# Multi-query attention on one core: value products dealt out one by one, more exponentials on VectorE, and part of their last product on GpSimd

## The chip, the cores and the metric

The kernel runs on one core of one Trainium2 chip. The metric is device time in microseconds (us) from start to end of one execution; smaller is better. The core has five engines that matter here: TensorE (PE in the profile; its weight loads are PEld), VectorE (DVE), ScalarE (ACT), GpSimd (POOL) and the queue engine SyncE (SP). Each runs its own list of instructions in order and waits on semaphores for the others.

## The reference

Sixteen query heads share one head of keys and values (batch 8, sequence 1024, head size 64).

```python
q: (8, 1024, 16, 64)   k, v: (8, 1024, 64)      # float32, random normal
scores  = q @ k.T / sqrt(64)                    # for every head
weights = softmax(scores, axis=-1)
out     = weights @ v                           # (8, 1024, 16, 64) float32
```

## The kernel before

The work is cut into steps. A step is one tile of scores: 128 keys (key tile `j`, 8 of them) by 512 queries (chunk `c`, 2 of them) for a pair of heads (`p`, 64 pairs over all batches), so 64 x 2 x 8 = 1024 steps. The tile is 128 partitions (keys) by 1024 columns (2 heads x 512 queries) and lies in PSUM, in one of three buffers `sc`. In each step `scores` has PE make the tile with two matmuls, and then one of two engines takes its exponential:

- ScalarE, in one instruction (line 260), into a float16 tile `wt`.
- VectorE, in every fifth step (`to_vector`, `VE_EVERY = 5`), in a unit of five instructions (`vector_exp`). The first (line 211) reads the scores from PSUM and writes an int16 whose bits, read as float16, are a straight-line approximation of the power. The next ones, from and to SBUF, take its mantissa `m` (line 217) and its power of two (line 227), square the mantissa (line 235, into `m2`) and multiply (line 237) the approximation by that square. The result is three tiles in one buffer `w3` (six buffers), which are added up by PE with values that are scaled by three constants. So a ScalarE tile needs one value product for each group of queries and a VectorE tile three.

The value products are in `values`: for a group `g` of 128 queries of one head (8 groups to a block of 8 steps, 1024 groups in all) it emits all products of that group over the 8 key tiles at once, 8 and two more for each VectorE tile among them. Seven groups share a PSUM bank. When a bank is full, `inverse` (line 263, reciprocal of the sums) and `finish` (line 272, scaling, then a store to memory) are put on the list `late`, and from there at the head of VectorE's list `pend`.

The order is written out by hand. The main loop runs over batches of two steps: for both steps scores and exponential, with two instructions taken from `pend` after each step; then the products of two groups whose tiles were made at least 16 steps before (`LAG`); then the loads and preparations for later batches (`after`). The last product of a unit (line 237) is held in `product` and joins `pend` behind the first instruction of the next unit. From step `HURRY` on (12 steps from the end) up to four groups follow each batch. `last_values` makes the products of the very last block, key tile by key tile, when all else is emitted.

GpSimd issues the loads of q (line 121) and v (line 104), and twice per batch of the input scales and converts K (line 190). SP issues K loads, transposes of q and K, and the stores.

Of the kernel before, what the change touches and what calls it, by code (L numbers as in the profile page):

```python
# [14 lines left out]
ALU = mybir.AluOpType  # L15
# [6 lines left out]
C0 = 0.9833984375  # L22
C3 = 0.163818359375
CS = 2.1471603163479376
VE_EVERY = 5


@with_exitstack
def attention_main(ctx, tc, q, k, v, out, flag):
# [11 lines left out]
    nc = tc.nc  # L41
    B, S, H, D = q.shape
    P = 128
    NKT = S // P
    QCH = 512
    NCH = S // QCH
    HP = H // 2
    NP = B * HP
    NQB = QCH // P
    GRP = 2 * NQB  # L50
    NG = NP * NCH * GRP
    GB = 7
# [15 lines left out]
    op = ctx.enter_context(tc.tile_pool(name="op", bufs=2, space=PSUM))  # L68
# [9 lines left out]
    kv = {}  # L78
    q16 = {}
    qt = {}  # L80
    wt = {}
    osb = {}
    ot = {}
    pend = []
    product = []
    late = []
# [48 lines left out]
    def bank(name):  # L135
        return op.tile([P, 512], FP32, tag="ot", name=name)
# [69 lines left out]
    def vector_exp(sc, p, c, j):  # L206
        w3 = w3p.tile([P, 3, 2, QCH], FP16, tag="w3", name=f"we{p}_{c}_{j}")
        m = mp.tile([P, 2, QCH], FP16, tag="m", name=f"m{p}_{c}_{j}")
        m2 = mp.tile([P, 2, QCH], FP16, tag="m2", name=f"mm{p}_{c}_{j}")
        t = w3[:, 1].bitcast(I16)  # L210
        nc.vector.tensor_scalar(  # L211
            out=t, in0=sc, scalar1=15.0 * 1024, scalar2=0.0, op0=ALU.add, op1=ALU.max
        )
        if product:
            pend.append(product.pop())
        pend.append(
            lambda: nc.vector.tensor_scalar(  # L217
                out=m.bitcast(I16),
                in0=t,
                scalar1=0x3FF,  # L220
                scalar2=0x3C00,
                op0=ALU.bitwise_and,
                op1=ALU.bitwise_or,
            )
        )
        pend.append(
            lambda: nc.vector.tensor_scalar(  # L227
                out=w3[:, 0].bitcast(I16),
                in0=t,
                scalar1=0x7C00,  # L230
                scalar2=None,
                op0=ALU.bitwise_and,
            )
        )
        pend.append(lambda: nc.vector.tensor_tensor(out=m2, in0=m, in1=m, op=ALU.mult))  # L235
        product.append(
            lambda: nc.vector.tensor_tensor(out=w3[:, 2], in0=w3[:, 1], in1=m2, op=ALU.mult)  # L237
        )
        wt[(p, c, j)] = [(w3[:, 0], 1), (w3[:, 1], 0), (w3[:, 2], 2)]

# [21 lines left out]
    def inverse(o, g0, n):  # L262
        nc.vector.reciprocal(out=rec_all[:, g0 : g0 + n], in_=o[:, 0:n, D])  # L263

    def finish(o, g0, n):

        rec = rec_all[:, g0 : g0 + n]
        i0 = g0 % (OCH * GRP)
        if i0 == 0:
            osb[0] = osbp.tile([P, OCH * GRP, D], FP32, tag="osb", name=f"osb{g0}")  # L270
        ob = osb[0]
        nc.vector.tensor_tensor(  # L272
            out=ob[:, i0 : i0 + n, :],
            in0=o[:, 0:n, 0:D],
            in1=rec.unsqueeze(2).broadcast_to([P, n, D]),
            op=ALU.mult,
        )
        while stored[0] < g0 + n:
            e = stored[0]
            e += GRP // 2 if e >= NG - GRP else GRP  # L280
            if e > g0 + n:
                break
            store(ob, stored[0], e)
            stored[0] = e
        per = HP * NCH * GRP
        if g0 + n == NG:
            check(g0 - GRP // 2, NG, ok_all[:, B:])
        elif checked[0] < B and g0 + n >= min((checked[0] + 1) * per, NG - GRP):
            e = min((checked[0] + 1) * per, NG - GRP)
            b = checked[0]  # L290
            check(b * per, e, None, ok_all[:, b : b + 1])
            checked[0] += 1

    def store(ob, g0, g1):
        p, c = divmod(g0 // GRP, NCH)
        b, hp = divmod(p, HP)
        q0 = c * QCH + g0 % GRP // 2 * P
        j0 = g0 % (OCH * GRP)
        n = g1 - g0
        nc.sync.dma_start(  # L300
            out=out[b, q0 : q0 + n // 2 * P, 2 * hp : 2 * hp + 2, :].rearrange(
                "(qb p) h d -> p qb (h d)", p=P
            ),
            in_=ob[:, j0 : j0 + n, :].rearrange("p (qb h) d -> p qb (h d)", h=2),
        )

    def values(p, c, g):

        b = p // HP
        qb, hh = divmod(g, 2)  # L310
        gg = (p * NCH + c) * GRP + g
        if gg % GB == 0:
            ot[0] = bank(f"ot{gg}")[:, 0 : GB * 72].rearrange("p (g f) -> p g f", f=72)
        o = ot[0]
        vp = kv[b]["vp"]
        terms = [(j, w, i) for j in range(NKT) for w, i in wt[(p, c, j)]]
        for n, (j, w, i) in enumerate(terms):
            nc.tensor.matmul(  # L318
                o[:, gg % GB, 0 : D + 1],
                w[:, hh, qb * P : (qb + 1) * P],  # L320
                vp[:, i, j, 0 : D + 1],
                start=(n == 0),
                stop=(n == len(terms) - 1),
            )
        if gg % GB == GB - 1 or gg == NG - GRP - 1:
            late.append((o, gg - gg % GB, gg % GB + 1))
        if g == GRP - 1:
            for j in range(NKT):
                del wt[(p, c, j)]

    def last_values():

# [39 lines left out]
    LAG = 2 * NKT + 2  # L372
    STEPS = NP * NCH * NKT
    PSTEPS = NCH * NKT
    BATCH = 2
    LAST_VE = (STEPS - 2 * NKT) // VE_EVERY * VE_EVERY
    HURRY = STEPS - NKT - 4

    def to_vector(u):
        return u % VE_EVERY == 0 and NKT <= u <= LAST_VE  # L380

    def step(u):
        p, r = divmod(u, PSTEPS)
        c, j = divmod(r, NKT)
        scores(p, c, j, to_vector(u))
        for _ in range(2):
            if pend:
                pend.pop(0)()
        if product and u >= LAST_VE + 2 and not pend:
            product.pop()()  # L390

    def after(u):
        p, r = divmod(u, PSTEPS)
# [24 lines left out]
    with tc.manual_schedule():  # L418
        load_kv(0)
        load_q_first(0)  # L420
        make_identity(nc, ident)
        for p in range(1, NFIRST):
            load_q_first(p)
        load_v(0)
        for c in range(NKT):
            load_q(0, c)
        for t in vps:
            for i, ci in enumerate((1.0, C0, C3)):
                nc.gpsimd.memset(t[:, i, :, D : D + 1], ci)
        nc.vector.tensor_copy(out=ident16, in_=ident)  # L430
        nc.vector.memset(ones, 1.0)
        kps = bank("kps0").bitcast(FP16)
        turned[0] = bank("qps0").bitcast(FP16)
        lo, hi = range(NKT // 2), range(NKT // 2, NKT)
        q0 = q16[("first", 0)]
        nc.scalar.copy(out=q0[:, 0 : NKT // 2, :], in_=qf[:, 0 : NKT // 2, :])  # L436
        first_k(kps, 0)
        first_q(turned[0], 0, lo)
        first_q_out(turned[0], 0, lo, nc.scalar.copy)
        first_k_out(kps, 0)  # L440
        first_k(kps, 1)
        first_k_out(kps, 1)
        nc.vector.tensor_copy(out=q0[:, NKT // 2 :, :], in_=qf[:, NKT // 2 :, :])
        prep_v(0)
        for c in range(NKT):
            turn_q(0, c)
        nxt = 0
        for u0 in range(0, STEPS, BATCH):
            us = range(u0, u0 + BATCH)
            for u in us:  # L450
                step(u)
            for f in late:
                pend.insert(0, lambda f=f: inverse(*f))
                pend.insert(min(2, len(pend)), lambda f=f: finish(*f))
            del late[:]
            for _ in range(2 * BATCH):
                if u0 < HURRY:
                    ready = nxt < u0 + BATCH - LAG
                else:
                    ready = nxt < STEPS - GRP and nxt // GRP * NKT + NKT + 4 <= u0  # L460
                if ready:
                    pa, ra = divmod(nxt, PSTEPS)
                    values(pa, *divmod(ra, NKT))
                    nxt += 1
            for u in us:
                after(u)
        assert nxt == STEPS - GRP
        assert not product
        for f in pend:
            f()  # L470
        for f in late:
            inverse(*f)
            finish(*f)
        last_values()
        okm = chkp.tile([P, 1], FP32, tag="okm", name="okm")
        nc.vector.tensor_reduce(out=okm, in_=ok_all, axis=AX.X, op=ALU.min)
        cnt = bank("cnt")[0:1, 0:1]
        nc.tensor.matmul(cnt, okm, ones, start=True, stop=True)
        nc.vector.tensor_scalar(
            out=flag, in0=cnt, scalar1=P - 0.5, scalar2=None, op0=ALU.is_lt  # L480
        )
# [120 lines left out]
```

## Time and profile before

| | us |
|---|---|
| median of 3 runs | 782.24 (781.58 to 783.35) |
| the profiled execution | 783.46 |
| its span, first to last instruction | 781.5 |

| engine | busy us | share of the span |
|---|---|---|
| PE | 728.7 | 93% |
| VectorE | 728.9 | 93% |
| ScalarE | 762.5 | 98% |
| GpSimd | 65.9 | 8% |

A group's row names line, engine and operation, what is written from what, the number of instructions, their busy time and the mean duration of one, and behind the second bar the engine's idle time just before them with what ended it. In the timeline a row begins with start and duration. VectorE's instructions overlap at their edges, so a mean is longer than the distance from one start to the next. The PE clock granted was 0.99 over the run.

### The profile page before, as it was taken

What the parts mean: (1) busy time and instruction counts of PE and PEld (TensorE: products, weight loads), DVE (VectorE), ACT (ScalarE), POOL (GpSimd) and SP (SyncE); (2) the same over time, 40 slices, a digit from 0 to 9 for tenths busy, and PEclk for the clock granted to TensorE, in tenths of its full rate; (3) what the DMA queues carried; (4) which work ended last, traced back from release to release, by engine and by line L of the source; (5) the groups of instructions that cost most, each with busy time, mean ns of one, the idle gap of its engine ahead of it and who ended that gap; (6) DMA issues with size and microseconds to landing.
All of it is one profiled execution on the core that took longest, in us unless ns stands there. A gap on an engine that the chain in (4) does not pass through costs nothing.

```text
span 781.5 us, 30669 instructions
## 1 busy us (share of the span) xinstructions
PE 728.7 (93%) x13474; PEld 474.1 (61%) x13474; DVE 728.9 (93%) x1349; ACT 762.5 (98%) x827; POOL 65.9 (8%) x99
## 2 busy tenths in 40 slices
PE   5999999999999999999999999999999999999996
PEld 2566666656666666666656666666666666666665
DVE  3899999999999999999999999999999999999992
ACT  7999999999999999999999999999999999999996
POOL 4210002100011002010020100201002100000000
PEclk8899999999999999999999999999999999999999
DMA  9949118582193813756155552556417373111113
GB/s 169 146 93 164 55 44 157 97 136 57 29 170 76 154 33 76 150 103 115 45 91 123 124 95 56 90 128 115 101 42 125 89 149 71 51 35 55 43 43 84
DMA packets 168633, 73.84 MB, mean 94 GB/s; under 512 B 93744, under 2 KB 161328, under 8 KB 168496
## 3 DMA queue, kind: packets, MB, share of 16 engines
q1 hardware_dynamic: 148864, 53.76, 32.5%
q0 software_dynamic: 18576, 17.57, 14.8%
q8 instruction: 106, 1.74, 1.0%
q10 hardware_dynamic: 1056, 0.52, 0.3%
q14 instruction: 31, 0.25, 0.1%
HBM read 37.75 MB, written 33.55 MB: 91 GB/s over the span
## 4 chain that ended last, share of the span: by engine, by line
ACT 38%; DVE 21%; PE 21%; issue 19%; DMA 1%; DVEq 0%; ACTq 0%
ACT wt L260 38%; PE ot L318 11%; PE sc L247 9%; DVE we L211 8%; DVE osb L272 3%; DVE we L237 3%; DVE mm L235 3%; DVE m L217 2%; DVE we L227 2%; DVE rec_all L263 1%; DMA qf<-in_q_dram 1%; PE otl L344 0%; DVE both L366 0%; DVE ok_all L370 0%; DVE ge L360 0%
## 5 line engine op out<-in xcount | busy, mean ns | idle before, releaser
L260 ACT ACTIVATE wt<-sc 128x1024 f16<-128x1024 f32 x824 | 760.0, 1062 | 7.4 <-PE sc L247 6.1
L318 PE MATMUL ot<-vp,wt 128*128 128x65 f16 x6528 | 418.4, 194 | 0.6 <-issue 0.6
L318 PEld LDWEIGHTS <-wt 128*128 128x128 f16 x6528 | 325.8, 98 | 114.8 <-issue 114.8
L247 PE MATMUL sc<-qt,k2t 64*128 64x512 f16 x2048 | 352.8, 386 | 41.2 <-ACT wt L260 29.1
L318 PE MATMUL ot<-vp,we 128*128 128x65 f16 x4800 | 352.2, 193 | 0.0
L318 PEld LDWEIGHTS <-we 128*128 128x128 f16 x4800 | 250.0, 97 | 30.6 <-issue 30.6
L211 DVE TENSOR_SCALAR we<-sc 128x1024 int16<-128x1024 f32 x200 | 243.6, 1218 | 23.2 <-PE sc L247 22.1
L247 PEld LDWEIGHTS <-k2t 64*128 64x128 f16 x2048 | 93.2, 94 | 149.0 <-issue 111.0
L237 DVE TENSOR_TENSOR we<-we,mm 128x1024 f16<-128x1024 f16 x200 | 136.9, 685 | 0.0
L235 DVE TENSOR_TENSOR mm<-m 128x1024 f16<-128x1024 f16 x200 | 136.5, 683 | 0.0
L272 DVE TENSOR_TENSOR osb<-ot,rec_all 128x448 f32<-128x448 f32 x146 | 90.5, 620 | 4.2 <-DVE rec_all L263 0.2
L217 DVE TENSOR_SCALAR m<-we 128x1024 int16<-128x1024 int16 x200 | 85.8, 429 | 0.0
L227 DVE TENSOR_SCALAR we<-we 128x1024 int16<-128x1024 int16 x200 | 83.5, 418 | 0.0
L104 POOL DMA_DIRECT2D vp<-in_v_dram x8 | 7.5, 936 | 388.5 <-PE ot L318 388.4
L121 POOL DMA_DIRECT2D q<-in_q_dram x64 | 35.0, 571 | 26.7 <-DMA qt<-q 22.9
L263 DVE RECIPROCAL rec_all<-ot 128x7 f32<-128x7 f32 x146 | 28.6, 196 | 8.7 <-PE ot L318 8.6
L190 POOL TENSOR_SCALAR k16d<-knat 128x512 f16<-128x512 f32 x14 | 21.4, 1537 | 134.7 <-DMA knat<-in_k_dram 134.7
L202 DVE TENSOR_SCALAR vp<-vp 128x512 f16<-128x512 f16 x16 | 3.9, 286 | 2.0 <-DMA vp<-in_v_dram 2.0
L155 PE MATMUL kps<-ident,k 128*64 128x128 f16 x16 | 1.3, 314 | 4.5 <-DVE k L146 4.5
L184 DVE COPY qt<-qps 128x512 f16<-128x512 f16 (+1 forms) x2 | 1.1, 554 | 3.3 <-PE qps L171 3.3
L155 PEld LDWEIGHTS <-k 128*64 128x64 f16 x16 | 0.8, 159 | 4.7 <-DVE k L146 4.7
L436 ACT ACT_TABLE_LOAD x1 | 1.3, 1283 | 1.9 <-issue 1.9
(29 smaller groups left out, 22.2 us busy)
## 6 DMA issues: line engine op xcount, KB each, us to landing
out_dram<-osb SPq DMA_DIRECT2D x127, 256.0 KB, 2.4
q<-in_q_dram POOLq DMA_DIRECT2D x56, 256.0 KB, 8.8
knat<-in_k_dram SPq DMA_DIRECT2D x7, 256.0 KB, 4.1
q<-in_q_dram POOLq DMA_DIRECT2D x8, 192.0 KB, 8.0
vp<-in_v_dram POOLq DMA_DIRECT2D x8, 128.0 KB, 4.4
qt<-q SPq DMA_TRANSPOSE x64, 3.9
qf<-in_q_dram ACTq DMA_DIRECT2D x2, 256.0 KB, 4.4
knat<-in_k_dram SPq DMA_DIRECT2D x2, 128.0 KB, 3.8
```

Of the source, the lines that this page charges most:

```text
L121: nc.gpsimd.dma_start(out=q16[(b, c)], in_=q[b, c * P : (c + 1) * P, h0:, :].rearrange("p h d -> p (h d)"),)
L190: nc.gpsimd.tensor_scalar(out=k16d[:, :, i, :], in0=st["knat"], scalar1=kscale, scalar2=None, op0=ALU.mult)
L211: nc.vector.tensor_scalar(out=t, in0=sc, scalar1=15.0 * 1024, scalar2=0.0, op0=ALU.add, op1=ALU.max)
L217: lambda: nc.vector.tensor_scalar(out=m.bitcast(I16), in0=t, scalar1=0x3FF, scalar2=0x3C00, op0=ALU.bitwise_and, op1=ALU.bitwise_or,)
L227: lambda: nc.vector.tensor_scalar(out=w3[:, 0].bitcast(I16), in0=t, scalar1=0x7C00, scalar2=None, op0=ALU.bitwise_and,)
L235: pend.append(lambda: nc.vector.tensor_tensor(out=m2, in0=m, in1=m, op=ALU.mult))
L237: lambda: nc.vector.tensor_tensor(out=w3[:, 2], in0=w3[:, 1], in1=m2, op=ALU.mult)
L247: nc.tensor.matmul(sc[:, hh, :], k2t[r : r + 64, j * P : (j + 1) * P], qt[b][r : r + 64, p % HP, c * QCH : (c + 1) * QCH], start=True, sto ...
L260: nc.scalar.activation(out=w, in_=sc, func=EXP, scale=escale, bias=math.log(CS))
L263: nc.vector.reciprocal(out=rec_all[:, g0 : g0 + n], in_=o[:, 0:n, D])
L272: nc.vector.tensor_tensor(out=ob[:, i0 : i0 + n, :], in0=o[:, 0:n, 0:D], in1=rec.unsqueeze(2).broadcast_to([P, n, D]), op=ALU.mult,)
L318: nc.tensor.matmul(o[:, gg % GB, 0 : D + 1], w[:, hh, qb * P : (qb + 1) * P], vp[:, i, j, 0 : D + 1], start=(n == 0), stop=(n == len(terms ...
```

## The change

- Units: of 41 steps 9 go to VectorE, so 4 or 5 steps lie between units (5 before); there are 220 in place of 200, up to step 1007 (1005 before).
- The last product of a unit is split by columns. VectorE keeps the first 384 of 1024. The other 640 go to GpSimd, in an instruction that is issued with the square and waits for it.
- The value products are dealt one by one. `values` now returns a list of single products; `plan` works out how many should have been emitted after each batch: more after a batch with two ScalarE tiles (about 35), fewer after one with a VectorE tile (about 9), with a correction of an eighth towards the group that is due. A group may begin two steps earlier than before (`AHEAD`), and its products may go over from one batch to the next. Before, a batch had two whole groups, 20 or 24 products.
- When one bank is finished, the first waiting entry of `pend` stands between its reciprocal and its scaling, as before.
- The end: `HURRY` begins 14 steps before the end (12 before), and a block may follow 2 steps earlier, so that the last batch of steps has no products behind it.

```diff
-VE_EVERY = 5
+VE_U = 384
+VE_N = 9
+VE_M = 41
...
-        pend.append(lambda: nc.vector.tensor_tensor(out=m2, in0=m, in1=m, op=ALU.mult))
+        we, wu, mm = (x.rearrange("p h q -> p (h q)") for x in (w3[:, 1], w3[:, 2], m2))
+
+        def square():
+            nc.vector.tensor_tensor(out=m2, in0=m, in1=m, op=ALU.mult)
+            nc.gpsimd.tensor_tensor(
+                out=wu[:, VE_U:], in0=we[:, VE_U:], in1=mm[:, VE_U:], op=ALU.mult
+            )
+
+        pend.append(square)
         product.append(
-            lambda: nc.vector.tensor_tensor(out=w3[:, 2], in0=w3[:, 1], in1=m2, op=ALU.mult)
+            lambda: nc.vector.tensor_tensor(
+                out=wu[:, :VE_U], in0=we[:, :VE_U], in1=mm[:, :VE_U], op=ALU.mult
+            )
         )
...
-    def values(p, c, g):
+    def values(gg):
...
-        for n, (j, w, i) in enumerate(terms):
+        def one(n, j, w, i):
+            last = n == len(terms) - 1
             nc.tensor.matmul(
...
+        return [lambda n=n, t=t: one(n, *t) for n, t in enumerate(terms)]
...
-    LAST_VE = (STEPS - 2 * NKT) // VE_EVERY * VE_EVERY
-    HURRY = STEPS - NKT - 4
+    OTHER = 21
+    AHEAD = 2
+    LAST_VE = max(u for u in range(STEPS - 2 * NKT + 1) if u * VE_N % VE_M < VE_N)
+    HURRY = STEPS - NKT - 6
 
     def to_vector(u):
-        return u % VE_EVERY == 0 and NKT <= u <= LAST_VE
+        return NKT <= u <= LAST_VE and u * VE_N % VE_M < VE_N
...
+    def plan():
+        at = range(LAG, HURRY, BATCH)
+        tiles = [sum(not to_vector(u) for u in range(u0, u0 + BATCH)) for u0 in at]
+        upto = [0]
+        for g in range(HURRY - LAG + AHEAD):
+            many = sum(to_vector(g // GRP * NKT + j) for j in range(NKT))
+            upto.append(upto[-1] + NKT + 2 * many)
+        each = (upto[HURRY - LAG] + OTHER * len(tiles)) / sum(tiles)
+        due, done = {}, 0.0
+        for u0, n in zip(at, tiles):
+            done += each * n - OTHER
+            done += (upto[u0 + BATCH - LAG + 1] - done) / 8
+            due[u0] = round(done)
+        return due
...
             for f in late:
-                pend.insert(0, lambda f=f: inverse(*f))
-                pend.insert(min(2, len(pend)), lambda f=f: finish(*f))
+                new += [lambda f=f: inverse(*f), lambda f=f: finish(*f)]
+            if len(new) == 2:
+                new[1:1] = pend[:1]
+                del pend[:1]
+            pend[:0] = new
             del late[:]
-            for _ in range(2 * BATCH):
-                if u0 < HURRY:
-                    ready = nxt < u0 + BATCH - LAG
-                else:
-                    ready = nxt < STEPS - GRP and nxt // GRP * NKT + NKT + 4 <= u0
-                if ready:
-                    pa, ra = divmod(nxt, PSTEPS)
-                    values(pa, *divmod(ra, NKT))
-                    nxt += 1
+            if u0 < HURRY:
+                while made < due.get(u0, 0):
+                    if not todo:
+                        if nxt >= u0 + BATCH + AHEAD - LAG:
+                            break
+                        todo = values(nxt)
+                        nxt += 1
+                    todo.pop(0)()
+                    made += 1
+            else:
+                for _ in range(2 * BATCH):
+                    if not todo and nxt < STEPS - GRP and nxt // GRP * NKT + NKT + 2 <= u0:
+                        todo = values(nxt)
+                        nxt += 1
+                    for f in todo:
+                        f()
+                    todo = []
```

More of the change, by code (lines that the diff above doesn't have):

```diff
@@ L305, in store @@
         )
-    def values(p, c, g):
-        b = p // HP
+    def values(gg):
+        p, c = divmod(gg // GRP, NCH)
+        g = gg % GRP
         qb, hh = divmod(g, 2)
-        gg = (p * NCH + c) * GRP + g
         if gg % GB == 0:
@@ L314, in values @@
         o = ot[0]
-        vp = kv[b]["vp"]
+        vp = kv[p // HP]["vp"]
         terms = [(j, w, i) for j in range(NKT) for w, i in wt[(p, c, j)]]
-        for n, (j, w, i) in enumerate(terms):
+        def one(n, j, w, i):
+            last = n == len(terms) - 1
             nc.tensor.matmul(
@@ L322, in values @@
                 start=(n == 0),
-                stop=(n == len(terms) - 1),
+                stop=last,
             )
[L325 to L329, printed above, removed]
+            if not last:
+                return
+            if gg % GB == GB - 1 or gg == NG - GRP - 1:
+                late.append((o, gg - gg % GB, gg % GB + 1))
+            if g == GRP - 1:
+                for x in range(NKT):
+                    del wt[(p, c, x)]
+        return [lambda n=n, t=t: one(n, *t) for n, t in enumerate(terms)]
     def last_values():
@@ L446, in attention_main @@
             turn_q(0, c)
-        nxt = 0
+        nxt = made = 0
+        todo = []
+        due = plan()
         for u0 in range(0, STEPS, BATCH):
@@ L451, in attention_main @@
                 step(u)
+            new = []
             for f in late:
-                pend.insert(0, lambda f=f: inverse(*f))
-                pend.insert(min(2, len(pend)), lambda f=f: finish(*f))
-            del late[:]
-            for _ in range(2 * BATCH):
-                if u0 < HURRY:
-                    ready = nxt < u0 + BATCH - LAG
-                else:
-                    ready = nxt < STEPS - GRP and nxt // GRP * NKT + NKT + 4 <= u0
-                if ready:
-                    pa, ra = divmod(nxt, PSTEPS)
-                    values(pa, *divmod(ra, NKT))
-                    nxt += 1
+                new += [lambda f=f: inverse(*f), lambda f=f: finish(*f)]
[3 more added lines that the diff above has]
+            pend[:0] = new
+            del late[:]
+            if u0 < HURRY:
[14 more added lines that the diff above has]
+                        f()
+                    todo = []
             for u in us:
```

## The prediction

> **What bounds the kernel now.** I read the page first: the shares of busy time, the chain that ended last, and the costliest groups.
>
> ```profile
> span 781.5 us, 30669 instructions
> PE 728.7 (93%) x13474; PEld 474.1 (61%) x13474; DVE 728.9 (93%) x1349; ACT 762.5 (98%) x827; POOL 65.9 (8%) x99
> ...
> ACT 38%; DVE 21%; PE 21%; issue 19%; DMA 1%; DVEq 0%; ACTq 0%
> ...
> L260 ACT ACTIVATE wt<-sc 128x1024 f16<-128x1024 f32 x824 | 760.0, 1062 | 7.4 <-PE sc L247 6.1
> L211 DVE TENSOR_SCALAR we<-sc 128x1024 int16<-128x1024 f32 x200 | 243.6, 1218 | 23.2 <-PE sc L247 22.1
> L237 DVE TENSOR_TENSOR we<-we,mm 128x1024 f16<-128x1024 f16 x200 | 136.9, 685 | 0.0
> L235 DVE TENSOR_TENSOR mm<-m 128x1024 f16<-128x1024 f16 x200 | 136.5, 683 | 0.0
> L272 DVE TENSOR_TENSOR osb<-ot,rec_all 128x448 f32<-128x448 f32 x146 | 90.5, 620 | 4.2 <-DVE rec_all L263 0.2
> L227 DVE TENSOR_SCALAR we<-we 128x1024 int16<-128x1024 int16 x200 | 83.5, 418 | 0.0
> L190 POOL TENSOR_SCALAR k16d<-knat 128x512 f16<-128x512 f32 x14 | 21.4, 1537 | 134.7 <-DMA knat<-in_k_dram 134.7
> L202 DVE TENSOR_SCALAR vp<-vp 128x512 f16<-128x512 f16 x16 | 3.9, 286 | 2.0 <-DMA vp<-in_v_dram 2.0
> ```
>
> ScalarE sets the pace: 824 tiles of 760.0 / 824 = 0.922 us, and only 7.4 us of idle between them. The chain is a mixture (ACT 38%, DVE 21%, PE 21%), which is what several nearly full engines look like. So the middle stretch comes next, in the view of stretches.
>
> ```profile
> 100.00:740.00 640.00, 607.69 (x11357) 397.39 (x11355) 619.31 (x1139) 635.09 (x690) 50.02 (x66) 1.00 0.46 92
> ```
>
> The columns after the length are PE, PEld, DVE, ACT and POOL. ScalarE is busy 635.09 / 640 = 99.2%, VectorE 619.31 / 640 = 96.8%, GpSimd 7.8% at most. A gain must come from fewer ScalarE tiles, and VectorE has about 3% to take them with.
>
> **What a VectorE unit costs.** Instructions overlap at their edges, so the price is the distance from start to start, read in the timeline; the rows also show GpSimd working beside VectorE, which decides this case.
>
> ```profile
> 143.15 1.22 DVE L211 TENSOR_SCALAR we<-sc 128x1024 int16<-128x1024 f32 x1 [0.24 <-PE sc L247]
> 144.29 0.68 DVE L237 TENSOR_TENSOR we<-we,mm 128x1024 f16<-128x1024 f16 x1
> 144.89 0.42 DVE L217 TENSOR_SCALAR m<-we 128x1024 int16<-128x1024 int16 x1
> 145.20 2.94 POOL L190 TENSOR_SCALAR k16d<-knat 128x512 f16<-128x512 f32 x2 [22.38 <-DMA knat<-in_k_dram]
> 145.23 0.86 DVE L227 TENSOR_SCALAR we<-we 128x1024 int16<-128x1024 int16 x1
> 146.01 0.68 DVE L235 TENSOR_TENSOR mm<-m 128x1024 f16<-128x1024 f16 x1
> 146.61 0.19 DVE L263 RECIPROCAL rec_all<-ot 128x7 f32<-128x7 f32 x1
> 146.84 0.62 DVE L272 TENSOR_TENSOR osb<-ot,rec_all 128x448 f32<-128x448 f32 x1
> 147.38 1.22 DVE L211 TENSOR_SCALAR we<-sc 128x1024 int16<-128x1024 f32 x1
> ...
> 332.33 2.94 POOL L190 TENSOR_SCALAR k16d<-knat 128x512 f16<-128x512 f32 x2 [18.86 <-DMA knat<-in_k_dram]
> 332.84 1.21 DVE L211 TENSOR_SCALAR we<-sc 128x1024 int16<-128x1024 f32 x1
> 333.97 0.97 DVE L237 TENSOR_TENSOR we<-we,mm 128x1024 f16<-128x1024 f16 x1
> 334.87 0.69 DVE L217 TENSOR_SCALAR m<-we 128x1024 int16<-128x1024 int16 x1
> 335.48 0.41 DVE L227 TENSOR_SCALAR we<-we 128x1024 int16<-128x1024 int16 x1
> 335.80 0.68 DVE L235 TENSOR_TENSOR mm<-m 128x1024 f16<-128x1024 f16 x1
> ```
>
> Undisturbed: the read of the scores (L211) 1.14, last product (L237) 0.60, L217 0.34, L227 0.32, square (L235) 0.60: 3.00 us. Reciprocal and scaling of a finished bank (L263, L272): 146.61 to 147.38 = 0.77.
>
> *The lock.* L227 takes 0.86 instead of 0.42 when it starts just after a GpSimd operation (0.44 late, until 145.67, 0.47 after GpSimd's start). The second operation at 332 starts at 332.33 + 1.47 = 333.80: L237 is held until 334.26 (0.46 after that start), and L217 until 335.14 (1.34 after). But L235 at 146.01 runs in its plain 0.68 while the first GpSimd operation has 0.66 us to go, and L211, L263 and L272, which read PSUM, never stretch. I read it so: GpSimd holds VectorE's SBUF operations while it reads, and the single-source ones (L217, L227) again while it writes, until 0.13 us before its end. Reads of PSUM go on beside it.
>
> **The change part by part.**
>
> *Fewer ScalarE tiles.* 220 units instead of 200: ScalarE loses 20 x 0.922 = 18.4 us.
>
> *VectorE's work.* The last product shrinks from 1024 to 384 columns. No row has it; L202 at 512 columns (286) against L227 at 1024 (418) leaves 154 ns fixed, so L237 has (685 - 154) / 1024 = 0.519 ns a column and 640 columns save 0.33 us: 0.27 remain. In pure proportion 0.60 x 384 / 1024 = 0.23, the lower bound; if nothing were saved 0.60 remain, 73 us in all, the upper. I take 0.27: L202 against L227 shows a part that does not shrink with the columns, but a small one. A unit costs 2.67.
>
> The first and the last unit of the 200:
>
> ```profile
> 15.49 1.22 DVE L211 TENSOR_SCALAR we<-sc 128x1024 int16<-128x1024 f32 x1 [1.26 <-PE sc L247]
> ...
> 756.73 1.22 DVE L211 TENSOR_SCALAR we<-sc 128x1024 int16<-128x1024 f32 x1
> ```
>
> 756.73 - 15.49 = 741.2 us is what ScalarE allowed VectorE between them. VectorE's own work in it was 199 x 3.00 + 142 x 0.77 + some 6 for the checks = 712. Afterwards: 219 x 2.67 + 142 x 0.77 + 6 = 700, plus what GpSimd's lock costs. ScalarE will allow 778 tiles x 0.922 = 717 for the same steps (10 to 1007, less 219 units), so each unit may lose 0.08 us before VectorE takes over the pace.
>
> *GpSimd's product, the disputed price.* No row shows a two-input product there. In bytes per partition it moves 3 x 1280 = 3840. L190 moves 2048 + 1024 in 1.47 us: 1.84 us. The other GpSimd row that reads SBUF moves 1024 bytes in 291 ns: 1.09 us.
>
> ```profile
> masks.py:199 POOL TENSOR_SCALAR_AFFINE_SELECT ident<-ident 128x128 f32<-128x128 f32 x1 | 0.3, 291 | 0.1
> ```
>
> I take the middle, 1.47, because L190 converts and writes in runs of 64 while the select does neither; both ends stay in the range. The Trainium skill, page "GPSIMD Engine Reference", section 3.1, has about 2.6 cycles an element for two-input operations, by which 640 columns would be an estimated 1.39 us; the forecast would be the same, and no run here shows it yet.
>
> *Where it falls.* It starts when the square has landed: 0.08 after the next VectorE instruction's start (146.69 against 146.61). For GpSimd's dispatch no row has a price; I allow 0.1, so 0.2 into what follows (each 0.1 more is like 0.1 on the product). Counting the emission order through: in 125 of 220 units (57%) the next unit's L211 follows at once, in 94 a bank's 0.77 us stand between. Both read PSUM and go beside GpSimd. After L211 come the small product and L217, at 0.94 and 1.21 us after GpSimd's start (0.77 later in the other 43%). With 1.47 us the lock ends at 1.34: 0.13 late in 57% of units, 0.07 on average. VectorE: 700 + 220 x 0.07 = 716, against ScalarE's 717. Both are then full.
>
> *What else is moved or queued.* On GpSimd's queue the products now stand between the K conversion (2.94 us, seven times) and the DMA issues of q and v; these no longer run ahead but come in step order. v is loaded 40 steps ahead of its first use, some 29 us; q 16 steps ahead of its transpose. A product behind a K conversion comes up to 2.9 us late, seven times, and then hits VectorE: about 1 us each at worst. SP's queue is untouched. A VectorE buffer of three tiles is reused every sixth unit, and the last matmul that reads it stands at least 2 steps ahead of that unit's scores in PE's own order (5 before), so no new wait. The third term of a unit is first used 6 steps or more after the unit whose instructions its product stands behind (7 before); PE runs at most 3 ahead, so 3 steps (2.2 us) cover the 1.41 to the small product's end.
>
> *PE.* 320 more products. A batch of two steps:
>
> ```profile
> 408.36 0.61 PE L247 MATMUL sc<-qt,k2t 64*128 64x512 f16 x4
> 408.90 0.27 PE L318 MATMUL ot<-vp,we 128*128 128x65 f16 x3
> 409.74 0.70 PE L247 MATMUL sc<-qt,k2t 64*128 64x512 f16 x4
> ```
>
> Scores 0.54, then 24 products in 0.84, 0.035 each. The new mean of 22.8 gives 1.34 us against 2 x 0.72 = 1.44 of ScalarE's new pace: hidden, with 7% to spare. Dealt singly, batches with two ScalarE tiles get about 35 products (0.54 + 1.22 = 1.76 of 1.84 us), those with one about 9 (0.86 of 0.92), where before they got 20 or 24 whatever ScalarE did. What that can win is ScalarE's wait for scores, 6.1 us at most.
>
> *The end.* The last block now has nothing but scores before it.
>
> ```profile
> 768.39 5.61 ACT L260 ACTIVATE wt<-sc 128x1024 f16<-128x1024 f32 x6
> ...
> 773.64 2.33 PE L344 MATMUL otl<-vp,wt 128*128 128x65 f16 x64 [0.84 <-DVE osb L272]
> ...
> 775.89 0.18 DVE L263 RECIPROCAL rec_all<-otl 128x4 f32<-128x4 f32 x1 [1.21 <-PE otl L344]
> ```
>
> ScalarE ends at 774.0, the 64 products at 775.9, held for a bank. With the batch before them empty, only the 8 products of the last tile follow ScalarE (0.28, and some 0.2 of drain): 1.4 us less.
>
> *Sum.* 781.5 - 18.4 - 1.4 = 761.7, if ScalarE's idle stays 7.4 us. With VectorE as full as ScalarE it won't: I add 6, nearly as much again, the delayed products behind the conversions included. Span 767.7. The profiled execution took 783.46 for a span of 781.5, 1.2 over the median of 782.24; from the median the same difference gives **768.4 us**.
>
> **The rivals.**
>
> *GpSimd is slow and VectorE paces (slower).* At L190's rate, 1.84 us, the lock ends at 1.71, L217 is 0.50 late in 57% of units: 700 + 220 x 0.285 = 763 instead of 741: 782.24 + 22 - 1.4 = 803 us. It decides from 700 + 220 x 0.57 x delay = 741, a delay of 0.33 or a product of 1.67 us. For it: L190 is the only long row and has one input less. Against: its time is mostly not bytes, as the select shows.
>
> *Half of it.* A product of 1.55 to 1.65: VectorE needs 726 to 739 and the time is 772 to 780.
>
> *The lock covers the whole operation.* The Trainium skill, page "SBUF — State Buffer", section "Who interferes with whom", says that a VectorE operation in a two-port mode or with two SBUF inputs and a GpSimd operation exclude each other for the whole instruction. As a mechanism here: with 1.47 us the small product waits 0.53 in 57% of units, 0.30 on average: 700 + 66 = 766, and 806 us. The undelayed L235 at 146.01 speaks against it in this trace; the held L227, L237 and L217 fit both.
>
> *ScalarE's tiles go but the pace stays* (PE's order or the score buffers hold it): 782. PE's 7% speak against it.
>
> **How the numbers follow.** Forecast 0.57, half 0.13, slow product 0.15, whole lock 0.09, pace stays 0.06. Faster by over 0.2% (1.6 us, about what a measurement of this kernel can tell) 0.70, within it 0.06, slower 0.24. Low end: no added idle and ScalarE's 6.1 us of waits gone give 756; I take 759. High end 793, between the flip and 803. The forecast's own range is 759 to 772.
>
> **What would show it.** The L260 group with 804 tiles and some 741 us; GpSimd's new group near 1.47 us; the first single-source instruction after the small product no more than 0.1 us above 429 ns in the mean, the square's row unchanged; ScalarE's idle 10 to 14 us; PE's wait of 0.84 ahead of the last products gone. The forecast is wrong if GpSimd's group is above 1.67 us, or if the small product itself is stretched, or if ScalarE waits for scores that wait for VectorE.

## The result: slower by a tenth

| | before | changed |
|---|---|---|
| median, us | 782.27 (781.58 to 783.35, 6 runs) | 859.68 (855.38 to 863.43, 6 runs) |
| ratio, 95% interval | | 1.098 (1.0945 to 1.1016) |
| span of the profiled execution, us | 781.5 | 858.4 |

The forecast was 768.4 us, a gain of 14; the change lost 77, far beyond the range. The page of the changed kernel, busy times and the groups that answer to those shown of before:

```profile
PE 746.8 (87%) x13794; PEld 474.7 (55%) x13794; DVE 743.6 (87%) x1449; ACT 766.5 (89%) x807; POOL 376.0 (44%) x319
...
L272 ACT ACTIVATE wt<-sc 128x1024 f16<-128x1024 f32 x804 | 764.0, 1026 | 82.0 <-PE sc L259 79.7
L241 POOL TENSOR_TENSOR we<-we,mm 128x640 f16<-128x640 f16 x220 | 307.5, 1398 | 462.1 <-DVE mm L240 264.3
L259 PE MATMUL sc<-qt,k2t 64*128 64x512 f16 x2048 | 356.5, 390 | 84.6 <-DVE we L213 52.0
L213 DVE TENSOR_SCALAR we<-sc 128x1024 int16<-128x1024 f32 x220 | 268.4, 1220 | 87.6 <-PE sc L259 87.2
L247 DVE TENSOR_TENSOR we<-we,mm 128x384 f16<-128x384 f16 x220 | 100.4, 457 | 0.0
L219 DVE TENSOR_SCALAR m<-we 128x1024 int16<-128x1024 int16 x220 | 94.3, 429 | 0.0
```

No engine is full any more. ScalarE has its 20 tiles less, but waits 82.0 us for scores where it waited 7.4, VectorE waits 87.6, and PE waits 84.6 for buffers that the two hold. Each waits for the others in turn. ScalarE's busy time rose too, although it has fewer tiles (764.0 us): a tile that starts after a wait does not overlap its predecessor (576 of 803 tiles start before the one ahead has ended, 785 of 823 before), so the time per tile is 764.0 / 804 = 0.950 against 0.922.

Of ScalarE's 207 waits for scores, 191 are at most half a microsecond long and make 53 us; three are of 6.06, 5.55 and 2.27 us. These are two different things.

**The short waits.** The timeline of the changed kernel, scores on PE, L213 and L247 on VectorE, and ScalarE; PE's value products, which lie between the score rows, are left out:

```profile
229.24 0.39 PE L259 MATMUL sc<-qt,k2t 64*128 64x512 f16 x2
229.92 0.35 DVE L247 TENSOR_TENSOR we<-we,mm 128x384 f16<-128x384 f16 x1
230.06 0.39 PE L259 MATMUL sc<-qt,k2t 64*128 64x512 f16 x2 [0.43 <-DVE we L213]
...
231.55 0.61 PE L259 MATMUL sc<-qt,k2t 64*128 64x512 f16 x4
...
232.23 1.21 DVE L213 TENSOR_SCALAR we<-sc 128x1024 int16<-128x1024 f32 x1
232.26 2.85 ACT L272 ACTIVATE wt<-sc 128x1024 f16<-128x1024 f32 x3 [0.35 <-PE sc L259]
...
233.50 0.39 PE L259 MATMUL sc<-qt,k2t 64*128 64x512 f16 x2 [0.64 <-DVE we L213]
234.99 0.61 PE L259 MATMUL sc<-qt,k2t 64*128 64x512 f16 x4
...
235.49 2.85 ACT L272 ACTIVATE wt<-sc 128x1024 f16<-128x1024 f32 x3 [0.37 <-PE sc L259]
```

A score tile waits for the buffer that VectorE still reads (0.43, then 0.64 us), and in those moments PE stands, since its list is in order. Only then come the 35 products of that batch, so that the next scores start 1.49 us after (230.06 to 231.55, 233.50 to 234.99), and ScalarE has run dry by then (0.35 and 0.37).

**The long waits.** Shortly before 185 us PE stops, and from 186 to 188 us no compute engine does anything. GpSimd's q loads, SP's transposes of q, PE's products, and a view by stretches (PE, PEld, DVE, ACT, POOL, granted clock, DMA share, GB/s):

```profile
168.18 1.26 POOL L123 DMA_DIRECT2D q<-in_q_dram  x2
...
171.81 1.27 POOL L123 DMA_DIRECT2D q<-in_q_dram  x2
...
177.00 15.01 SPq L133 DMA_TRANSPOSE qt<-q  x4
...
189.84 0.22 PE L333 MATMUL ot<-vp,wt 128*128 128x65 f16 x1 [5.11 <-issue]
```

```profile
184.00:186.00 2.00, 0.73 (x24) 0.64 (x21) 0.05 (x1) 1.58 (x2) 1.39 (x1) 1.00 1.28 128
186.00:188.00 2.00, 0.00 (x0) 0.00 (x0) 0.00 (x0) 0.00 (x0) 0.00 (x0) 0.97 1.21 119
188.00:190.00 2.00, 0.16 (x3) 0.02 (x3) 0.00 (x0) 0.00 (x0) 0.00 (x0) 0.50 1.17 140
190.00:192.00 2.00, 2.00 (x19) 1.00 (x20) 1.34 (x2) 0.87 (x1) 0.00 (x0) 0.50 2.10 225
```

PE waits 5.11 us for nothing that the profile shows, while the DMA engines are full. In the DMA records 81 packets took over 1.7 us, up to 6.10 (before: 10, at most 3.42, and that one in the start-up), loads and transposes alike. The instruction queue q8 brings packets of 16 KB, and their number goes with PE's products (106 with 13474 matmuls, 107 with 13618, 108 with 13794), so I read them as PE's code. They start 7 to 8 us apart as a rule; here two of them lie 16.3 us apart, and PE goes on 2.3 us after the late one. The other stop of this run, 5.39 us up to 75.0, has the same mark: 16.3 us between two code packets, and PE goes on 2.3 us after the second. So PE probably stood for want of code. Its clock then fell to 0.50 for 6.8 us. The Trainium skill, "TensorE: Matmul & The Clock Gate", section "Why this matters for your kernels", warns of idle gaps over about 3 us. This trace agrees for the gap of 5.1 us, but less can be enough: after a wait of 1.84 us, up to 719.95, the clock was at 0.50 for 3.4 us as well. Before, loads and transposes of the same q lay 29 us apart:

```profile
118.56 4.26 POOL L121 DMA_DIRECT2D q<-in_q_dram  x8
...
151.82 7.46 SPq L131 DMA_TRANSPOSE qt<-q  x5
```

### The profile page after: what moved, and what is told of

The parts are those of the page before. It is cut to its first block, busy times and chain, and to the rows that moved or that the text cites. A ratio compares the mean times of both kernels' runs of the same rounds, so it can differ in the third digit from the quotient of the medians.

```text
span 858.4 us, 31963 instructions
## 1 busy us (share of the span) xinstructions
PE 746.8 (87%) x13794; PEld 474.7 (55%) x13794; DVE 743.6 (87%) x1449; ACT 766.5 (89%) x807; POOL 376.0 (44%) x319
## 4 chain that ended last, share of the span: by engine, by line
PE 46%; DVE 33%; ACT 14%; issue 5%; DMA 0%; ACTq 0%; DVEq 0%
PE ot L333 28%; PE sc L259 17%; DVE we L213 17%; ACT wt L272 14%; DVE mm L240 5%; DVE osb L284 4%; DVE m L219 3%; DVE we L247 2%; DVE rec_all L275 1%; DVE we L229 1%; DVE vp L204 1%; DMA qf<-in_q_dram 0%; PE otl L363 0%; DVE both L385 0%; ACTq L272 0%
## 5 line engine op out<-in xcount | busy, mean ns | idle before, releaser
L272 ACT ACTIVATE wt<-sc 128x1024 f16<-128x1024 f32 x804 | 764.0, 1026 | 82.0 <-PE sc L259 79.7
L241 POOL TENSOR_TENSOR we<-we,mm 128x640 f16<-128x640 f16 x220 | 307.5, 1398 | 462.1 <-DVE mm L240 264.3
L259 PE MATMUL sc<-qt,k2t 64*128 64x512 f16 x2048 | 356.5, 390 | 84.6 <-DVE we L213 52.0
L333 PE MATMUL ot<-vp,we 128*128 128x65 f16 x5280 | 384.5, 193 | 1.1 <-DVE osb L284 1.0
L213 DVE TENSOR_SCALAR we<-sc 128x1024 int16<-128x1024 f32 x220 | 268.4, 1220 | 87.6 <-PE sc L259 87.2
L333 PEld LDWEIGHTS <-we 128*128 128x128 f16 x5280 | 283.0, 97 | 76.1 <-issue 75.8
L259 PEld LDWEIGHTS <-k2t 64*128 64x128 f16 x2048 | 80.7, 94 | 186.9 <-issue 159.1
L240 DVE TENSOR_TENSOR mm<-m 128x1024 f16<-128x1024 f16 x220 | 150.2, 683 | 0.1
L247 DVE TENSOR_TENSOR we<-we,mm 128x384 f16<-128x384 f16 x220 | 100.4, 457 | 0.0
L219 DVE TENSOR_SCALAR m<-we 128x1024 int16<-128x1024 int16 x220 | 94.3, 429 | 0.0
L229 DVE TENSOR_SCALAR we<-we 128x1024 int16<-128x1024 int16 x220 | 92.0, 418 | 0.0
L192 POOL TENSOR_SCALAR k16d<-knat 128x512 f16<-128x512 f32 x14 | 22.5, 1618 | 0.0
L204 DVE TENSOR_SCALAR vp<-vp 128x512 f16<-128x512 f16 x16 | 7.0, 476 | 1.5 <-DMA vp<-in_v_dram 1.5
```

Of the source, the lines that this page charges most:

```text
L213: nc.vector.tensor_scalar(out=t, in0=sc, scalar1=15.0 * 1024, scalar2=0.0, op0=ALU.add, op1=ALU.max)
L219: lambda: nc.vector.tensor_scalar(out=m.bitcast(I16), in0=t, scalar1=0x3FF, scalar2=0x3C00, op0=ALU.bitwise_and, op1=ALU.bitwise_or,)
L229: lambda: nc.vector.tensor_scalar(out=w3[:, 0].bitcast(I16), in0=t, scalar1=0x7C00, scalar2=None, op0=ALU.bitwise_and,)
L241: nc.gpsimd.tensor_tensor(out=wu[:, VE_U:], in0=we[:, VE_U:], in1=mm[:, VE_U:], op=ALU.mult)
L247: lambda: nc.vector.tensor_tensor(out=wu[:, :VE_U], in0=we[:, :VE_U], in1=mm[:, :VE_U], op=ALU.mult)
L259: nc.tensor.matmul(sc[:, hh, :], k2t[r : r + 64, j * P : (j + 1) * P], qt[b][r : r + 64, p % HP, c * QCH : (c + 1) * QCH], start=True, sto ...
```

## The experiments

All are cut from the changed kernel; times are medians against the kernel before on the same chip (782.36, 782.11 and 782.42 us on the three chips that were used).

**Whole groups again.**

```diff
-                while made < due.get(u0, 0):
-                    ...
+                while nxt < u0 + BATCH - LAG:
+                    for f in values(nxt):
+                        f()
+                    nxt += 1
```

> The changed kernel with the value products again dealt as two whole groups to each batch of two steps; the 220 units, the split product and the shorter end stay. Theory D (the dealing: blocks of some 35 products stand behind a pair of scores that waits for VectorE's buffer, ScalarE runs dry): the 191 short waits of ScalarE (53 us) fall to under 15, time 805 to 822 us. Rival V (GpSimd's lock and 220 units overfill VectorE, whatever the dealing): 845 us or more, VectorE busy over 97% in the middle. Rival Q (the loads of q now meet the transposes) alone would leave it at 855 to 863.

816.38 us, ratio 1.041 (1.0354 to 1.0466).

```profile
L272 ACT ACTIVATE wt<-sc 128x1024 f16<-128x1024 f32 x804 | 752.5, 1038 | 51.1 <-PE sc L259 47.4
```

The dealing is worth 43.3 us. 65 short waits remain (19.5 us, where under 15 was expected). VectorE is busy 95% of the middle, not over 97% as rival V had it.

**The dealing alone.** `VE_N, VE_M = 1, 5`, `VE_U = 1024`, no GpSimd product.

> The kernel before with the dealing alone (and the shorter end): every fifth step on VectorE, the whole last product on VectorE, nothing added on GpSimd, so loads run ahead as before. Theory D: ScalarE waits for scores at nearly every unit, 0.2 us and more, 200 times: 815 to 835 us. Rivals V and Q: 779 to 784, since neither lock nor late loads are in it.

821.49 us, 1.0493 (1.0459 to 1.0527): 39 us lost with 200 units, no product on GpSimd and loads as early as before. ScalarE's idle time is 29.9 us (22.5 more than before), and its busy time rose by another 17, since tiles that start after a wait do not overlap. The waits are fewer than expected: 95 of over 0.15 us, where 200 were forecast. The time is the one that theory D gave, from both sides.

**Loads early.**

```diff
             if at == 0:
                 load_kv(b + 1)
+            early = at + PSTEPS + NKT
+            if early == 0:
                 load_v(b + 1)
-            if 0 <= at < 2 * NKT and at % 2 == 0:
-                load_q(b + 1, at // 2)
+            if 0 <= early < 2 * NKT and early % 2 == 0:
+                load_q(b + 1, early // 2)
```

> The changed kernel with the loads of v and q put 24 steps earlier in the program, so that they land ahead of the transposes. Theory Q (transposes and loads of q in flight together hold packets for up to 6 us, PE's code arrives late, PE stands still and loses its clock): no wait of ScalarE over 2 us, no packet over 2 us, 835 to 848 us. Rivals D and V: the long waits are a small part, 853 us or more.

846.18 us, 1.081 (1.0775 to 1.0846). The longest wait of ScalarE is 2.19 us and one packet took over 2 us (2.03), both just over what theory Q allowed, and the clock stayed at 1.00 from the start-up to the end. 13.5 us were the late loads.

**The split alone.** `VE_N, VE_M = 1, 5`, whole groups.

> The kernel before with the split product alone (640 columns on GpSimd) and the shorter end: every fifth step on VectorE, whole groups. ScalarE keeps 824 tiles. Theory D: nothing lost in the middle but what late loads cost: 780 to 800 us. Rival V: the lock stretches VectorE's instructions by more than the 0.33 us saved: 800 us or more. Theory Q: one to three ScalarE waits over 2 us remain, 10 to 20 us of it.

797.91 us, 1.0182 (1.0113 to 1.0251), with ScalarE waits of 5.89, 3.68 and 2.38 us, and 73 packets over 2 us. Theories D and Q both allow this time. That it is the loads, moved in GpSimd's order by the split, is shown by the run with 200 units below: with early loads 14.0 us of it are gone.

**220 units, split and shorter end, without the dealing and the late loads.**

> The changed kernel with whole groups dealt as before and with the loads of v and q 24 steps earlier: what is left of the change are 220 units, the split product and the shorter end. If dealing and loads were all that went wrong, the prediction's own sum holds: 764 to 772 us. If the lock and the fuller VectorE cost as well (theory V as a third part): the first such run (816) less its long waits (25 us) and their slow clock (6): 780 to 792 us, with VectorE over 97% busy in the middle.

804.38 us, 1.0282 (1.026 to 1.0303): worse than both figures expected. VectorE is over 97% busy in the middle, as theory V had it (622.65 of 640 us), but the loss is larger: more than 20 us against the same with 200 units, which comes next.

```profile
100.00:740.00 640.00, 597.52 (x11288) 395.18 (x11288) 622.65 (x1188) 610.57 (x653) 308.72 (x250) 0.99 0.47 91
...
L272 ACT ACTIVATE wt<-sc 128x1024 f16<-128x1024 f32 x804 | 752.7, 1038 | 35.9 <-PE sc L259 32.4
L213 DVE TENSOR_SCALAR we<-sc 128x1024 int16<-128x1024 f32 x220 | 267.9, 1218 | 19.1 <-PE sc L259 17.4
L247 DVE TENSOR_TENSOR we<-we,mm 128x384 f16<-128x384 f16 x220 | 106.8, 486 | 0.0
L219 DVE TENSOR_SCALAR m<-we 128x1024 int16<-128x1024 int16 x220 | 93.0, 423 | 0.0
```

The small product takes 0.35 us in 56% of units and mostly 0.70 in the rest, 0.49 in the mean; L219 behind it is not held in the mean (423).

**The same with 200 units.**

> The kernel before with the split product, the shorter end and the loads of v and q 24 steps earlier; 200 units, whole groups. Theory Q: the 16 us that the split cost without early loads were long waits and slow clock: 773 to 780 us, no wait over 1.5 us. If the split itself costs (lock), 785 us or more.

783.93 us, 1.0021 (1.0011 to 1.003), above the range expected by 4.

```profile
100.00:740.00 640.00, 604.46 (x11324) 398.25 (x11320) 583.18 (x1137) 631.83 (x688) 291.64 (x237) 1.00 0.46 92
```

VectorE is busy 583.18 of 640 us in the middle, 91% against 97% before, and nothing comes of it, as ScalarE has its 824 tiles again. ScalarE's longest wait is 1.93 us, where at most 1.5 was expected.

**Even amounts, still singly.** `done += upto[HURRY - LAG] / len(tiles)` in place of `each * n - OTHER`, loads early.

> As the changed kernel with early loads (846 us), products still dealt one by one and groups begun two steps earlier, but the same number (some 23) after every batch, whatever ScalarE has in it. If the uneven amounts (35 and 9) are what costs: 780 to 798 us. If dealing singly, across batches or earlier costs by itself: 820 us or more.

800.73 us, 1.0246 (1.0215 to 1.0278), 3 above the range expected: 45 us better than the same with 35 and 9 (846.18), and no worse than whole groups (804.38). Dealing singly is harmless; the uneven amounts were the loss.

**Amounts turned round.** 8 added after a batch with one ScalarE tile, 6.3 taken off with two.

> As the run with even single products and early loads (800.7 us), but with the amounts turned round: about 31 products after a batch with a VectorE tile and 16 after one with two ScalarE tiles. Theory D says that products should stand where PE would otherwise wait for VectorE's buffer: as good or better, 792 to 802 us. If any unevenness costs, as 35 and 9 did: 820 us or more.

809.84 us, 1.0339 (1.0309 to 1.037): between the two forecasts. Filling the wait behind a VectorE tile is 36 us better than emptying it (though the amounts are 15 apart here and 26 there), and still 9 worse than even amounts, so that part of theory D fell.

**220 units without the split.**

> 220 units, whole groups, early loads, shorter end, but the whole last product on VectorE and none on GpSimd (1024 columns). VectorE's work from the first to the last unit is 219 x 3.00 + 142 x 0.77 + 6 = 772 us where 741 stood before: 806 to 816 us with VectorE near 99%. What lies between this and the run with the split is what the split gives back net of its lock; if the lock ate all of it, both would be equal.

817.56 us, 1.0448 (1.0426 to 1.0469), just above the range expected; VectorE is 99% busy in the middle (636.34 of 640 us) and sets the pace. The split takes 73 us of columns from VectorE (220 x 0.33). VectorE's own work from the first unit to the last, its waits taken out, falls by 31 of them (772 to 741 us), and 13 reach the time.

**512 columns on GpSimd.**

> As the run with 220 units, whole groups and early loads (804.4 us), but 512 columns on GpSimd. If the lock's hold on the small product (0.35 us in 41% of units) is what overfills VectorE: GpSimd's operation falls to some 1.1 us and ends its reading just as the small product comes; VectorE saves some 0.13 us a unit and pays 0.07 for 128 more columns: 788 to 798 us. If the lock doesn't matter, VectorE only has more to do: 810 to 820 us.

794.4 us, 1.0147 (1.0119 to 1.0176).

```profile
L241 POOL TENSOR_TENSOR we<-we,mm 128x512 f16<-128x512 f16 x220 | 254.3, 1156 | 447.6 <-DVE mm L240 185.5
L247 DVE TENSOR_TENSOR we<-we,mm 128x512 f16<-128x512 f16 x220 | 99.6, 453 | 0.0
```

128 more columns for VectorE, and L247 got shorter in the mean (486 to 453): the lock mattered, and 640 columns were too many for this order.

**Few units more.** 5 of 24 steps; the kernel has 209 units and 815 ScalarE tiles, one off the figures in the expectation.

> Whole groups, early loads, shorter end, 208 units (5 in 24 steps), and 512 instead of 640 columns of the last product on GpSimd. By the sum, ScalarE has 812 tiles: 12 x 0.922 = 11 us less than with 200 units (783.9), while VectorE, at 91% there, has room: 773 to 778 us. Rival: the uneven distance between units (4 or 5 steps) costs by itself with three score buffers: 782 us or more.

791.94 us, 1.0115 (1.0087 to 1.0143): the rival held. The distances from one L213 to the next in the timelines, means over the middle units, in us:

```
units  last product on GpSimd   4 steps apart   5 steps apart
209    512                      3.35            3.70
220    512                      3.33            3.55
220    640                      3.34            3.61
200    640                      -               3.73
ScalarE's own time              2.77            3.69
```

Four steps hold three ScalarE tiles, 3 x 0.922 = 2.77 us, and VectorE needs 3.35 for a unit there: 0.58 late. In the next five steps it has time to spare by its own work, but with 209 units ScalarE sets 3.70 for them, and the lost time isn't won back. Neither engine is full on average here: from the first unit to the last, VectorE's own work is 705 us and ScalarE's 790 tiles would need 728 (790 x 0.922), but 754 pass. That three score buffers are too few to carry the difference is argued from these distances; no run had more.

**The shorter end alone.**

> The kernel before with the shorter end alone (200 units, whole groups, whole last product on VectorE, loads as before). By the prediction 1.4 us less than before: 780.5 to 781.5 us, PE's wait of 0.84 us ahead of the last 64 products gone. Rival: nothing, 782 to 783, because the last group's work on VectorE is late instead.

781.26 us, 0.9982 (0.9967 to 0.9998): 1.2 us, as forecast. PE's wait fell from 0.84 to 0.30 us; it was to be gone. This is the only version that beats the kernel before, by less than this measurement can well tell.

```profile
771.23 2.35 PE L360 MATMUL otl<-vp,wt 128*128 128x65 f16 x64 [0.30 <-DVE osb L281]
```

## Why the prediction was wrong, by its own steps

The runs make a chain, each with one step more: 783.9 (split, early loads, shorter end), 804.4 (220 units), 816.4 (loads in step order), 859.7 (uneven dealing). So +1.6, +20.5, +12.0 and +43.3, together the 77.4 us that the change cost.

1. *"Dealt singly ... What that can win is ScalarE's wait for scores, 6.1 us at most."* This step failed most, by 43 us (42 with early loads, 804.4 against 846.2). I compared times (1.76 of 1.84 us, 0.86 of 0.92) and found PE hidden. I left out that a batch's products stand behind its scores in PE's list, and its scores wait for a buffer. It is the place of the work in the order that counts, not its sum. I had allowed no loss there, and the rival "the pace stays" was far too kind.
2. *"ScalarE will allow 778 tiles x 0.922 = 717 ... VectorE: 700 + 220 x 0.07 = 716, against ScalarE's 717. Both are then full."* The step from 200 to 220 units, forecast at -18.4 with 6 added for two full engines, measured +20.5. Two things were wrong. First, VectorE's 716 was too small: with early loads (804.4) its own work between the first and the last unit, waits taken out, is 741 us, already more than ScalarE's 717, and 22 us of waits come on top. Of the 25 us, 14 are the hold of point 3 and 6 are L204, the preparation of v, which takes 9.9 us in place of the 3.9 of L202 before. Second, it is a mean over 41 steps. It fits only if a unit that is late by 0.58 us in four steps can take the time from the next five. With 209 units, where both engines have room on average, that did not happen. With 512 columns in place of 640 on GpSimd 10 us came back (804.4 against 794.4).
3. *"With 1.47 us the lock ends at 1.34: 0.13 late in 57% of units"*, for L217. The price was near: 1.398 us. It was taken as the middle of two rates, so that is partly luck. By the Trainium skill, "GPSIMD Engine Reference", section 3.1, which has 2.6 cycles an element, it would be an estimated 1.39 us, and this trace agrees for 640 columns. The rival of the slow product is out. The place was wrong. I took the reading of two inputs to be as short as that of L190's one input (0.47 us), so that only L217 (L219 now) would be held. But it is the small product that is held, until nearly the end, one of the signs that the prediction had named for its being wrong:

```profile
409.27 1.22 DVE L213 TENSOR_SCALAR we<-sc 128x1024 int16<-128x1024 f32 x1
409.49 1.40 POOL L241 TENSOR_TENSOR we<-we,mm 128x640 f16<-128x640 f16 x1 [2.34 <-PE ot L333]
410.40 0.70 DVE L247 TENSOR_TENSOR we<-we,mm 128x384 f16<-128x384 f16 x1
411.03 0.41 DVE L219 TENSOR_SCALAR m<-we 128x1024 int16<-128x1024 int16 x1
```

   GpSimd starts 0.22 into L213, as worked out. L247 is 0.35 late, to 410.75, 1.26 after GpSimd's start. With 220 units, whole groups and early loads 44% of the small products are held (57% were counted), 0.14 us on average over all units (486 against 349 ns), 30 us of VectorE's time instead of 16; in the changed kernel itself, with its many waits, 33% and 0.11 us. So the rival "the lock covers the whole operation" had named the right instruction, at twice the price. The Trainium skill, page "SBUF — State Buffer", section "Who interferes with whom", says that whoever issues first has the shared ports for the whole instruction. For two inputs this trace agrees but for the last 0.14 us; for one input it does not: in the trace of before, L237 was held until some 0.47 us after GpSimd's start at 333.80, and L235 at 146.01, 0.81 after another such start, was not held.
4. *"q 16 steps ahead of its transpose."* I asked whether the data would be there in time. I did not ask what the loads would meet on the DMA engines and put that at nothing: they ran into the transposes, and PE stood, probably for code that came late. Three pairs of runs with and without early loads give 12.0, 13.5 and 14.0 us, with the clock's fall.
5. *The small product at 0.27 us* came true where it is not held (403.46 to 403.73 in the changed kernel's timeline), and *the end*, 1.4 us, measured 1.2, with an interval from 0.2 to 2.6.

What stays open: that PE waited for code rests on the gaps in the code packets and on the waits' disappearance when the loads moved, not on a run in which the code alone was moved. In the run with whole groups and late loads, too, three stops of PE (3.33, 4.66 and 4.05 us) end 2.2 to 2.4 us after a code packet that came 12.4 to 13.2 us behind the one before; but with 220 units and no split a gap of 12.1 us passed without a stop. Whether more score buffers would carry the uneven distances was not tried. Why amounts turned round cost 9 us more than even ones was not tried further.

## What to carry to other kernels

Where engines hand a few buffers round and each works its list in order, a budget of means is not enough: write down for the shortest distance between two units what each engine needs, and see whether the buffers carry the difference. Work that fills gaps must stand in the list where the gap is; the same work behind the wait makes the next engine starve. And a new instruction in a queue that used to run ahead moves everything behind it: ask not only whether those transfers are still in time, but what they now run beside.

## What the runs showed of the hardware

- GpSimd's product of two float16 tiles: 1398 ns for 640 columns and 1156 for 512, so 1.89 ns a column and some 0.19 us fixed.
- Its hold on VectorE's two-input SBUF operations ended 1.26 us after its start with 640 columns and 1.02 with 512, both 0.14 before its own end. With one input of 512 columns (1.47 us) it ended after 0.47, and a two-input VectorE operation that started later ran undelayed.
- Loads of q from GpSimd's queue and transposes from SP's, in flight together, held packets up to 6.10 us in the changed kernel and 7.04 in the run with whole groups; in the runs with the loads put earlier no packet after the start-up took over 2.35 us.
- TensorE's clock fell to 0.50 after stops of 5.11 us (for 6.8 us) and of 1.84 us (for 3.4 us), but after another stop of 1.84 us, up to 706.9 in the run with early loads, it did not.
